# Moving the gate rows, the mask and the second block's loads, and splitting one weight tile earlier

## The chip, the cores and the metric

The kernel runs on one core of a Trainium2 chip. The metric is device time in microseconds (us) of one execution. The core's engines work side by side, each through its own instructions in program order: TensorE (PE, matmuls), VectorE (DVE), ScalarE (ACT), GpSimd (POOL, idle here), and SyncE (SP), which issues the loads. An instruction waits for those of other engines through semaphores.

## What is computed

Two transformer blocks in sequence over 256 tokens of width 1024, in float32. The first block:

```python
h = rmsnorm(x, norm1_g[l])
(hg_q, hg_f, hg_i, hg_g, ml_qk, ml_v, ml_if, ml_o,
 mb_z, mb_xbc, mb_dt, gate_pre) = jnp.split(h @ w_in[l], split_at, axis=-1)
log_f = jnp.log(lb + (1.0 - lb) * jax.nn.sigmoid(hg_f))
o_hg = hgrn2_scan(jax.nn.silu(hg_q), log_f, hg_i)
qk = jax.nn.silu(causal_dwconv(ml_qk, ml_conv_w[l], ml_conv_b[l]))
log_f_m = jax.nn.log_sigmoid(ml_if[..., 4:] + gb[4:])
h_ml = mlstm_scan(q_m, k_m * (ML_DQK ** -0.5), v_m, ml_if[..., :4] + gb[:4], log_f_m)
dt = jax.nn.softplus(mb_dt + mb_dt_bias[l])
y_ssd = ssd_scan(xs, dt, A, Bm, Cm)
mixed = gates[0] * (y_hg @ w_br_hg[l]) + gates[1] * (y_ml @ w_br_ml[l]) + gates[2] * (y_mb @ w_br_mb[l])
x = x + mixed @ w_out[l]
u = causal_dwconv(rmsnorm(x, norm2_g[l]) @ w_up[l], ffn_conv_w[l], ffn_conv_b[l])
u_g, u_v = jnp.split(u, 2, axis=-1)
x = x + (jax.nn.silu(u_g) * u_v) @ w_down[l]
```

The second block (two layers) has a context of 256 further tokens, a modulation by a condition vector, three kinds of mixing (one of them attention in a window, which needs a mask) and a feed-forward of the same kind. It uses the first block's x; its context and its layer parameters do not depend on the first block.

## The kernel before

Activations stand transposed, features on partitions: eight tiles of 128 x 256. Every weight matrix is cut into tiles of 128 x 1024. A tile is loaded (raw, 512 KB, four buffers, issued by SP), rounded to a high half on ACT (wh, L393) and to the rest on DVE (wl, L395), with three buffers for each half. A product is then 24 matmuls of 128 x 256, in threes: high by high (L414), high weight by low activation (L416), low weight by high activation (L417); where the activations are the stationary side the three are L439 to L441 (psx).

In the order of the program (a scheduler then sorts the instructions by it and by what they wait for, and each engine keeps the order that results):

- The start: x is loaded, normed (`rms_feat`), and while the norm is not there yet the first three tiles (`small`, hf0, hf1) are multiplied with the gain-scaled x (gh, gl) and scaled afterwards (`scaled`, L747, u). `normed` (L732) makes h and splits it into xh and xl (L400, L401), which all later tiles use. `small` holds the gate columns of the mLSTM and of the SSD; U is made of them.
- `small_rows` (L786 to L801) makes softplus (SP) and its scan (CS) from U, with a series for the logarithm: two ACT instructions and 17 on DVE, each over 128 x 256. It is called after the first step of `proj_a`, and CS and SP are first used in the mLSTM and the SSD, long after. Behind it the window mask is loaded and cast to `winb` (L1214).
- `run_ratio` runs the projections `proj_a` (hq, hi), `proj_b` (mqk, mv, xbc) and `proj_c` with the first scan, `hgrn_core`, a step of each in turn. A step of `proj_b` for mqk is one weight tile, a convolution (`conv4`, L923: an ACT row and three DVE rows cv) and a silu (`silu2`, L837: mq or hq from a tanh th). A step of `hgrn_core` makes decays E (L879 to L886), four pairs of psl matmuls, and takes them into AT (L901).
- Then the branches, the output product and the first feed-forward: 22 pairs of up tiles (j from 0), each followed by a convolution (ag, av, L641), a silu and a product. Its first four tiles (j below `raws` = 2) are again multiplied with gain-scaled x and scaled later (u, L1363), after which `normed` makes XH and XL. `hook1(j)` is called after every j; from j = 9 it takes a step of `context_norm`: modulation steps, `prepare(0)` (tables of the second block's first layer from its parameters plt), the context's norm.
- Between the weights run the modulation's steps: weight-like tiles reduced on DVE (L596), and tiles multiplied on PE (psada, L551, L552) whose rows are copied (arow) and turned (psat, L538).

The context (ctxT, eight loads of 128 KB) is loaded ahead of the first block's last branch; plt (588 KB) in `prepare`, when its pool is free.

Of the kernel before, what the change touches and what calls it, by code (L numbers as in the profile page):

```python
# [287 lines left out]
class Knobs:  # L288
    raw = 4
# [17 lines left out]
def tile_two_blocks(ctx: ExitStack, tc: tile.TileContext, xT, ctxT, cst1, cst, cstw, pb1, pl0, pl1, pf0, pf1, pc, pcb, wb, w0, w1, out,  # L307
# [55 lines left out]
    def load_params(pool, spec, src, nm):  # L363
        off, n = _poffs(spec)
        t = pool.tile([128, n], F32, name=nm)
        nc.sync.dma_start(out=t, in_=src)
        return lambda k: t[:, off[k][0]:off[k][0] + off[k][1]]
# [253 lines left out]
    def ffn(ph, pool, halves, xh, xl, cw3, cb, causal, resid, hook=None, mid=None, raw=None, raws=1):  # L621
# [6 lines left out]
        def part(c):  # L628
            return lambda k: (xh[:, k, c], xl[:, k, c])
# [23 lines left out]
        for j0, j1 in CHUNKS:  # L653
            hid = []
            for j in range(j0, j1):
                if j == 0 and raw:

                    ks, ps, us = [(i, e) for i in range(raws) for e in range(2)], [], []
                    for i, k in enumerate(ks):
                        if i >= 3:  # L660
                            us.append(raw[1](ps[i - 3]))
                        ps.append(gemm_ws(ph, ("up",) + k, raw[0], raw[3]))
                    us += [raw[1](p) for p in ps[len(us):]]
                    raw[2]()
                    pg, pv = us[0:2]
                elif j < raws and raw:
                    pg, pv = us[2 * j:2 * j + 2]
                elif j == 0:

                    w = [weight(ph, ("up", e // 2, e % 2), 128) for e in range(3)]  # L670
                    first = [PS.g.tile([128, 512], F32, tag=PS.gtag, name="psg") for _ in range(3)]
                    for c in reversed(H):
                        for e, ps in enumerate(first):
                            mm3(ps[:, c], w[e], part(c), 8, True)
                    pg, pv, pg1 = first
                elif j == 1 and not raw:
                    pg = pg1
                else:
                    pg = gemm_ws(ph, ("up", j, 0), part(slice(0, n)), n)
# [10 lines left out]
                if hook:  # L690
                    hook(j)
# [60 lines left out]
    uf = [scaled(gemm_ws(0, ("hf", j), graw, 256)) for j in range(2)]  # L752
    normed(xh, xl, x, r, g1[:, 0:8])
    dump("h", xh)
# [9 lines left out]

    lbe = p1.tile([128, 8], F32, name="lbe")
# [3 lines left out]
    S.activation(out=lbe, in_=lbe, func=AF.Exp)  # L769
    lbs = p1.tile([128, 8], F32, name="lbs")  # L770
# [11 lines left out]
    def small_rows():  # L782

        z = mid.tile([128, 256], F32, tag="E", name="z", bufs=4)
        s = mid.tile([128, 256], F32, tag="E", name="s", bufs=4)
        s2 = mid.tile([128, 256], F32, tag="E", name="s2", bufs=4)  # L786
        p = mid.tile([128, 256], F32, tag="E", name="p", bufs=4)
# [143 lines left out]
    def proj_b():  # L931
        for j in range(8):
            ps = gemm_ws(0, ("mqk", j), rhs, 256)
            silu2(mq[:, j * 256:(j + 1) * 256], conv4(ps, P("mcw"), P("mcb"), j))
            yield
# [273 lines left out]
    small_rows()  # L1209
    V.tensor_copy(identb, ident)  # L1210
    V.tensor_copy(causb, C("causal"))
    win = mid.tile([128, 512], F32, tag="E", name="win", bufs=4)
    nc.sync.dma_start(out=win, in_=cstw)
    V.tensor_copy(winb.rearrange("p a b -> p (a b)"), win)  # L1214
# [48 lines left out]
    cx = load_x(res2, ctxT, tag="cx")  # L1263
# [15 lines left out]
    def prepare(i):  # L1279
# [3 lines left out]
        P = L.P = load_params(lp, _pl(i), (pl0, pl1)[i], "plt")  # L1283
# [61 lines left out]
    def context_norm():  # L1345
        ada_steps(max(0, 32 - Ada.done))
        LS[0] = prepare(0)
        yield
        r = rms_feat(cx)
        yield  # L1350
        yield from norm_steps(LS[0], cx, r, 0, 1)
# [3 lines left out]
    def hook1(j):  # L1355
        if j >= 9:
            next(cn, None)

# [38 lines left out]
    def layer(L):  # L1397
# [366 lines left out]
        else:  # L1764
# [7 lines left out]
            def hook(j):  # L1772
# [53 lines left out]
```

## Time and profile before

| | before |
|---|---|
| median of three runs | 1729.18 us |
| the runs | 1727.62 to 1729.49 us |
| the profiled execution | 1728.11 us |
| its span in the profile | 1726.3 us |
| granted TensorE clock, mean of the span | 0.991 |
| busy: PE, DVE, ACT | 1680.2, 1422.8, 943.0 us |
| DMA | 278 MB, 161 GB/s in the mean |

The span runs from the first to the last recorded instruction; 1.8 us of the execution lie outside it. PE is busy for 97% of the span, DVE for 82%. A busy share says little about a place: at each, what counts is which engine waits and what ended its wait.

### The profile page before, as it was taken

Reading aid. Unit: us, or ns where it says so; the run is one execution under the profiler, and the core shown is the slowest. Engines: PE = TensorE matmul, PEld = TensorE weight load, DVE = VectorE, ACT = ScalarE, POOL = GpSimd, SP = SyncE. Lnnn points to the kernel's source line nnn. Section 1 sums busy time; section 2 is a strip of 40 time slices with the busy share of each in tenths; the row PEclk is TensorE's granted clock in tenths of the full one; section 3 lists DMA queues with packets and bytes.
Section 4 is the critical chain, followed back from the end, with each engine's and each line's share of the span. In section 5 each row is a group of like instructions: output and inputs, shape, how many; then the busy total and the mean of one; then the engine's idle time right before and its main releaser. Section 6 shows DMA issues by size and latency. Waiting matters only on the chain.

```text
span 1726.3 us, 31575 instructions
## 1 busy us (share of the span) xinstructions
PE 1680.2 (97%) x12334; PEld 1529.8 (89%) x12334; DVE 1422.8 (82%) x2788; ACT 943.0 (55%) x1661; POOL 0.2 (0%) x4
## 2 busy tenths in 40 slices
PE   7999999999999999999999999999999998899999
PEld 7999998889898999989877988888888996799999
DVE  8987977668789987876788899999997868688776
ACT  7655644444456665666777553431244555576454
POOL 0000000000000000000000000000000000000000
PEclk9999999999999999999999999999999999999999
DMA  8545454536665677764311546657753542046564
GB/s 264 162 151 156 137 159 121 150 111 213 206 212 165 194 234 224 218 203 147 99 50 52 169 138 184 186 170 237 242 165 110 170 134 63 1 144 196 177 193 135
DMA packets 80645, 278.01 MB, mean 161 GB/s; under 512 B 9072, under 2 KB 13808, under 8 KB 80240
## 3 DMA queue, kind: packets, MB, share of 16 engines
q1 hardware_dynamic: 80496, 275.99, 52.1%
q8 instruction: 97, 1.59, 0.4%
q14 instruction: 52, 0.43, 0.1%
HBM read 274.91 MB, written 1.05 MB: 160 GB/s over the span
## 4 chain that ended last, share of the span: by engine, by line
PE 84%; DVE 10%; ACT 3%; DMA 2%; issue 1%; SPq 0%; ACTq 0%; DVEq 0%
PE psg L414 20%; PE psg L417 20%; PE psg L416 20%; PE psx L439 3%; PE psx L441 3%; PE psx L440 3%; DVE wl L395 3%; PE psc L1568 2%; PE psl L894 1%; PE psc L1607 1%; ACT wh L393 1%; PE pso L1629 1%; PE pso L1626 1%; DMA raw<-w 1%; ACT Pp L1587 1%
## 5 line engine op out<-in xcount | busy, mean ns | idle before, releaser
L393 ACT CAST wh<-raw 128x1024 fp32r<-128x1024 f32 (+1 forms) x439 | 453.3, 1037 | 514.3 <-PE psg L416 419.0
L395 DVE TENSOR_TENSOR wl<-raw,wh 128x1024 fp32r<-128x1024 f32 (+1 forms) x439 | 528.2, 1206 | 136.6 <-ACT wh L393 133.6
L414 PE MATMUL psg<-XH,wh 128*128 128x256 f32 (+1 forms) x1272 | 396.3, 314 | 4.7 <-ACT wh L393 3.8
L417 PE MATMUL psg<-XH,wl 128*128 128x256 f32 (+1 forms) x1272 | 395.0, 313 | 4.7 <-DVE wl L395 4.7
L416 PE MATMUL psg<-XL,wh 128*128 128x256 f32 (+1 forms) x1224 | 384.6, 315 | 0.9 <-DVE XL L1331 0.5
L414 PEld LDWEIGHTS psg<-XH,wh 128*128 128x128 f32 x1272 | 240.3, 190 | 23.3 <-ACT wh L393 5.9
L417 PEld LDWEIGHTS psg<-XH,wl 128*128 128x128 f32 x1272 | 240.6, 190 | 21.3 <-DVE wl L395 5.7
L416 PEld LDWEIGHTS psg<-XL,wh 128*128 128x128 f32 x1224 | 231.9, 190 | 17.6 <-issue 1.1
L414 PE MATMUL psg<-xh,wh 128*128 128x256 f32 x720 | 208.2, 289 | 1.3 <-ACT xh L400 1.3
L417 PE MATMUL psg<-xh,wl 128*128 128x256 f32 x720 | 205.3, 285 | 2.6 <-DVE wl L395 2.6
L416 PE MATMUL psg<-xl,wh 128*128 128x256 f32 x720 | 205.7, 286 | 0.6 <-DVE xl L401 0.6
L414 PE MATMUL psg<-hh,wh 128*128 128x256 f32 (+1 forms) x592 | 178.6, 303 | 0.2
L416 PE MATMUL psg<-hl,wh 128*128 128x256 f32 (+1 forms) x592 | 178.3, 302 | 0.0
L417 PE MATMUL psg<-hh,wl 128*128 128x256 f32 (+1 forms) x592 | 178.2, 302 | 0.0
L414 PEld LDWEIGHTS psg<-xh,wh 128*128 128x128 f32 x720 | 137.8, 191 | 4.9 <-issue 2.9
L417 PEld LDWEIGHTS psg<-xh,wl 128*128 128x128 f32 x720 | 137.7, 191 | 4.9 <-DVE wl L395 3.2
L416 PEld LDWEIGHTS psg<-xl,wh 128*128 128x128 f32 x720 | 138.1, 192 | 1.8 <-issue 1.0
L414 PEld LDWEIGHTS psg<-hh,wh 128*128 128x128 f32 x592 | 111.0, 188 | 7.3 <-ACT hh L400 1.1
L416 PEld LDWEIGHTS psg<-hl,wh 128*128 128x128 f32 x592 | 111.2, 188 | 5.7 <-DVE hl L401 0.2
L417 PEld LDWEIGHTS psg<-hh,wl 128*128 128x128 f32 x592 | 111.1, 188 | 5.1
L439 PE MATMUL psx<-wh,XH 128*128 128x256 f32 x384 | 110.2, 287 | 1.3 <-ACT wh L393 0.8
L441 PE MATMUL psx<-wl,XH 128*128 128x256 f32 x384 | 109.3, 286 | 0.6 <-DVE wl L395 0.4
(445 smaller groups left out, 3181.7 us busy)
## 6 DMA issues: line engine op xcount, KB each, us to landing
raw<-w SPq DMA_DIRECT2D x238, 512.0 KB, 4.1
raw<-wb SPq DMA_DIRECT2D x197, 512.0 KB, 4.3
araw<-w SPq DMA_DIRECT2D x56, 512.0 KB, 4.3
raw<-w SPq DMA_DIRECT2D x16, 384.0 KB, 3.3
raw<-wb SPq DMA_DIRECT2D x8, 384.0 KB, 4.0
xres<-xT SPq DMA_DIRECT2D x16, 128.0 KB, 4.3
ccb<-pcb SPq DMA_DIRECT2D x2, 1024.0 KB, 5.4
plt<-pl SPq DMA_DIRECT2D x2, 588.0 KB, 4.2
```

Of the source, the lines that this page charges most:

```text
L393: S.copy(wh[:, 0:sz], raw[:, 0:sz])
L395: V.tensor_tensor(wl[:, 0:sz], raw[:, 0:sz], wh[:, 0:sz], ALU.subtract)
L414: T.matmul(o, wh[:, k], xh, start=(first and k == 0), stop=False)
L416: T.matmul(o, wh[:, k], xl, start=False, stop=False)
L417: T.matmul(o, wl[:, k], xh, start=False, stop=(last and not late and k == nk - 1))
L439: T.matmul(o, xh, wh[:, k % 4], start=(k == 0), stop=False)
L440: T.matmul(o, xl, wh[:, k % 4], start=False, stop=False)
L441: T.matmul(o, xh, wl[:, k % 4], start=False, stop=(k == 7))
L894: T.matmul(ps[:, a, t], E[:, o:o + 128], E[:, o:o + 128], start=True, stop=True)
L1568: T.matmul(ps[e][:, 0:A.nk], q_[d, jq, A.tq], k_[d, jk, kk], start=(n == 0), stop=(n == 2 and not mask))
L1587: S.activation(out=p[:, 0:A.nk], in_=o, func=AF.Exp, scale=ss[:, A.t, h:h + 1], bias=nm, accum_out=sums[:, c:c + 1])
L1607: T.transpose(ps[:, n], p[:, b * 128:(b + 1) * 128], ident)
```

## The change

- The start: hf0 and hf1 are multiplied as before; hf1 is scaled only behind `normed`. A single sigmoid (`sg0`) is called before the others.
- `small_rows` is called in `proj_b`, at the fifth mqk tile, and takes its four tiles from the pool of tmp instead of mid.
- The window mask is loaded in two halves and cast in `hook1`, at j = 6 and 7.
- The context is loaded in `hook1` at j = 4, behind a small ACT copy that writes a column of its tile from av; plt likewise behind a small ACT copy.
- In the first feed-forward the weight tile of j = 2 (the fifth) is asked for before the first four products are scaled (`ahead`).
- `hook1` takes one modulation step more at j = 12, 15 and 18.

```diff
-    def load_params(pool, spec, src, nm):
+    def load_params(pool, spec, src, nm, gate=None):
+        if gate is not None:
+            S.copy(t[:, 0:1], gate[:, 0:1])
         nc.sync.dma_start(out=t, in_=src)
...
                         ps.append(gemm_ws(ph, ("up",) + k, raw[0], raw[3]))
+                    ahead = weight(ph, ("up", raws, 0), 128)
                     us += [raw[1](p) for p in ps[len(us):]]
                     raw[2]()
...
-                    pg = gemm_ws(ph, ("up", j, 0), part(slice(0, n)), n)
+                    pg = gemm_ws(ph, ("up", j, 0), part(slice(0, n)), n, w=ahead if raw and j == raws else None)
...
-    uf = [scaled(gemm_ws(0, ("hf", j), graw, 256)) for j in range(2)]
+    uf = [gemm_ws(0, ("hf", j), graw, 256) for j in range(2)]
+    uf[0] = scaled(uf[0])
     normed(xh, xl, x, r, g1[:, 0:8])
+    uf[1] = scaled(uf[1])
...
+    S.activation(out=sg0, in_=ones, func=AF.Sigmoid)
...
-        z = mid.tile([128, 256], F32, tag="E", name="z", bufs=4)
...
+        z, s, s2, p = (tmp.tile([128, 256], F32, tag="t256", name=nm, bufs=6) for nm in ("z", "s", "s2", "p"))
...
     def proj_b():
         for j in range(8):
+            if j == 4:
+                small_rows()
             ps = gemm_ws(0, ("mqk", j), rhs, 256)
...
     next(pa)
-    small_rows()
...
-    win = mid.tile([128, 512], F32, tag="E", name="win", bufs=4)
-    nc.sync.dma_start(out=win, in_=cstw)
-    V.tensor_copy(winb.rearrange("p a b -> p (a b)"), win)
...
-    cx = load_x(res2, ctxT, tag="cx")
+    cx = res2.tile([128, 8, 256], F32, name="xres", tag="cx")
...
-        LS[0] = prepare(0)
+        LS[0] = prepare(0, gate[0])
...
+    def hook1(j, av):
+
+        gate[0] = av
+        if j in (6, 7):
+            win = tmp.tile([128, 256], F32, tag="t256", name="win", bufs=6)
+            nc.sync.dma_start(out=win, in_=cstw[:, (j - 6) * 256:(j - 5) * 256])
+            V.tensor_copy(winb[:, j - 6], win)
+        if j == 4:
+            S.copy(cx[:, :, 0:1], av[:, 0:8].unsqueeze(2))
+            for k in range(8):
+                nc.sync.dma_start(out=cx[:, k], in_=ctxT[:, k])
         if j >= 9:
             next(cn, None)
+        if j in (12, 15, 18):
+            ada_steps(1)
```

What this does to the order on DVE is shown at three places. In the rows an operation stands with what it writes and reads; line numbers of the changed kernel are 3 to 6 higher. The first place is the start, from the wl of the third hf tile on, before:

```order
L395 TENSOR_TENSOR wl<-raw,wh 128x1024
L747 TENSOR_TENSOR u<-psg,rr 128x256 x2
L760 TENSOR_SCALAR U<-u,pb1t,ct_125 128x256
L747 TENSOR_TENSOR u<-psg,rr 128x256
L732 SCALAR_TENSOR_TENSOR h<-xres,g_126,rr 128x256 x4
L401 TENSOR_TENSOR xl<-h,xh 128x256 x4
```

and in the changed kernel:

```order
L398 TENSOR_TENSOR wl<-raw,wh 128x1024
L751 TENSOR_TENSOR u<-psg,rr 128x256 x2
L736 SCALAR_TENSOR_TENSOR h<-xres,g_126,rr 128x256 x4
L766 TENSOR_SCALAR U<-u,pb1t,ct_125 128x256
L398 TENSOR_TENSOR wl<-raw,wh 128x1024
L404 TENSOR_TENSOR xl<-h,xh 128x256 x4
```

The four h come ahead of U and of the third u, and the wl of the fourth hf tile, which stood 16 rows behind these h, comes ahead of xl.

The second place is DVE from the wl of the last mqk tile to the wl of the first mv tile (the two wl rows here), before:

```order
L395 TENSOR_TENSOR wl<-raw,wh 128x1024
L837 SCALAR_TENSOR_TENSOR mq<-th,cv 128x256
L923 SCALAR_TENSOR_TENSOR cv<-psg,pb1t,cv 128x253
L886 TENSOR_TENSOR E<-E,hq 128x64x4
L923 SCALAR_TENSOR_TENSOR cv<-psg,pb1t,cv 128x254
L884 TENSOR_TENSOR E<-hb 128x128x2
L923 SCALAR_TENSOR_TENSOR cv<-psg,pb1t,cv 128x255
L901 COPY_PREDICATED AT<-ct_125,psl 128x2x256
L923 SCALAR_TENSOR_TENSOR cv<-psg,pb1t,cv 128x253
L837 SCALAR_TENSOR_TENSOR mq<-th,cv 128x256
L923 SCALAR_TENSOR_TENSOR cv<-psg,pb1t,cv 128x254
L395 TENSOR_TENSOR wl<-raw,wh 128x1024
```

In the changed kernel there are 35 rows between the two, the 17 of `small_rows` among them; the last of them are:

```order
L802 SCALAR_TENSOR_TENSOR p<-p,s_1453 128x256
L929 SCALAR_TENSOR_TENSOR cv<-psg,pb1t,cv 128x254
L803 SCALAR_TENSOR_TENSOR p<-p,s 128x256
L929 SCALAR_TENSOR_TENSOR cv<-psg,pb1t,cv 128x255
L805 SCALAR_TENSOR_TENSOR SP<-p,z 128x256
L907 COPY_PREDICATED AT<-ct_125,psl 128x2x256
L806 TENSOR_SCALAR z<-SP,acol 128x256
L843 SCALAR_TENSOR_TENSOR mq<-th,cv 128x256
L807 SCALAR_TENSOR_TENSOR CS<-ct_125,z 128x256
L929 SCALAR_TENSOR_TENSOR cv<-psg,pb1t,cv 128x253
L892 TENSOR_TENSOR E<-E,hq 128x64x4
L398 TENSOR_TENSOR wl<-raw,wh 128x1024
```

The E row of the level 64, which four pairs of psl matmuls read, is now the last but one of the 35, where it was the third of ten.

The third place is DVE in the body of the first feed-forward, where the context's norm begins (sacc, rcy, rct are its rows), between two wl rows, before:

```order
L395 TENSOR_TENSOR wl<-raw,wh 128x1024
L401 TENSOR_TENSOR hl<-av,hh 128x256
L459 TENSOR_TENSOR rct<-rct,psn 128x2
L596 ISA raw,mod_93<-raw,ccb,pf_575 128x1024
L596 ISA mod_93 128x1
L461 SCALAR_TENSOR_TENSOR rcy<-rct,rcy 128x2
L641 SCALAR_TENSOR_TENSOR ag<-psg,pb1t,ag 128x254
L457 TENSOR_TENSOR rct<-rcy 128x2
L395 TENSOR_TENSOR wl<-raw,wh 128x1024
```

The same stretch of the changed kernel has 40 rows between the two wl (those marked x2 counted twice); it begins with

```order
L457 TENSOR_SCALAR rcy<-psn 128x2
L398 TENSOR_TENSOR wl<-raw,wh 128x1024
L644 SCALAR_TENSOR_TENSOR av<-psg,pb1t,av 128x254
L1279 TENSOR_SCALAR g5n1g<-plt 128x8
L1297 TENSOR_SCALAR gtbqn<-plt 128x64
L1297 TENSOR_SCALAR gtbkn<-plt 128x64
L1280 SCALAR_TENSOR_TENSOR gs<-mod_93,g5n1g 128x16
L1298 TENSOR_TENSOR ctbqn<-ct,gtbqn 128x128
L1304 TENSOR_TENSOR stbqn<-ct,gtbqn 128x4x16 x2
```

and all rows of `prepare` now stand in it; before, a first half of them stood ahead of the fifth up tile's wl and a second half four wl rows ahead of this place.

## Rows read from the trace of the kernel before

**Rows 1.** The page's part 4, the chain that ended last, share by engine.

```profile
PE 84%; DVE 10%; ACT 3%; DMA 2%; issue 1%; SPq 0%; ACTq 0%; DVEq 0%
```

**Rows 2.** Timeline of PE at the start: start, duration, instruction, [idle before <- what ended it].

```profile
21.98 0.50 PE L414 MATMUL psg<-xh,wh 128*128 128x256 f32 x2 [1.35 <-ACT xh L400]
...
29.31 0.39 PE L417 MATMUL psg<-xh,wl 128*128 128x256 f32 x1 [1.43 <-DVE wl L395]
...
53.35 1.16 PE L869 MATMUL psl<-hq,hk 128*128 128x128 f32 x8 [1.54 <-DVE hq L837]
```

**Rows 3.** Timeline of DVE and of ACT at the start.

```profile
21.02 1.66 DVE L732 SCALAR_TENSOR_TENSOR h<-xres,g,rr 128x256 f32<-128x256 f32 x4
...
52.54 0.43 DVE L1214 CAST winb<-win 128x512 bf16<-128x512 f32 x1 [0.72 <-DMA win<-cstw]
52.89 0.75 DVE L837 SCALAR_TENSOR_TENSOR hq<-th,psg 128x256 f32<-128x256 f32 x2
...
51.21 1.02 ACT L836 ACTIVATE th<-psg 128x256 f32<-128x256 f32 x3
```

**Rows 4.** Timeline of DVE, rows of `small_rows` at their place before.

```profile
31.27 1.74 DVE L791 RECIPROCAL s<-s 128x256 f32<-128x256 f32 x1
...
46.61 3.17 DVE L796 SCALAR_TENSOR_TENSOR p<-p,s 128x256 f32<-128x256 f32 x7
```

**Rows 5.** Timeline of DVE from the last mqk tile's wl to the first mv tile's.

```profile
118.57 1.22 DVE L395 TENSOR_TENSOR wl<-raw,wh 128x1024 fp32r<-128x1024 f32 x1
119.71 0.42 DVE L837 SCALAR_TENSOR_TENSOR mq<-th,cv 128x256 f32<-128x256 f32 x1
120.04 0.48 DVE L923 SCALAR_TENSOR_TENSOR cv<-psg,pb1t,cv 128x253 f32<-128x253 f32 x1
120.43 0.42 DVE L886 TENSOR_TENSOR E<-E,hq 128x256 f32<-128x256 f32 x1
...
121.96 0.75 DVE L901 COPY_PREDICATED AT<-ct,psl 128x512 f32<-128x512 uint32 x1
...
123.75 1.22 DVE L395 TENSOR_TENSOR wl<-raw,wh 128x1024 fp32r<-128x1024 f32 x1
```

**Rows 6.** Timeline of PE, the first instruction behind the last mqk tile.

```profile
128.32 1.05 PE L894 MATMUL psl<-E 128*128 128x128 f32 x8
129.13 0.36 PE L439 MATMUL psx<-wh,xh 128*128 128x256 f32 x1
```

**Rows 7.** Busy time by stretch; PEclk is the granted clock.

```profile
28.00:33.00 5.00, 3.69 (x31) 3.69 (x32) 5.00 (x10) 4.55 (x10) 0.00 (x0) 1.00 0.46 136
...
142.00:160.00 18.00, 18.00 (x153) 17.90 (x152) 9.58 (x14) 8.77 (x15) 0.00 (x0) 1.00 0.54 153
544.50:549.50 5.00, 4.60 (x26) 4.60 (x27) 5.00 (x10) 2.31 (x8) 0.00 (x0) 0.66 0.63 156
```

**Rows 8.** Timeline of PE at the first feed-forward's head and behind its body.

```profile
544.90 0.45 PE L417 MATMUL psg<-XH,wl 128*128 128x256 f32 x1 [2.97 <-DVE wl L395]
...
741.79 0.28 PE L538 MATMUL psat<-ct,arow 4*128 4x4 f32 x2 [1.37 <-ACT arow L563]
```

**Rows 9.** Timeline of DVE at that head: the fifth up tile's wl, the sixth's.

```profile
532.34 1.22 DVE L395 TENSOR_TENSOR wl<-raw,wh 128x1024 fp32r<-128x1024 f32 x1
533.48 0.75 DVE L1363 TENSOR_TENSOR u<-psg,rr 128x256 f32<-128x256 f32 x2
...
543.63 1.22 DVE L395 TENSOR_TENSOR wl<-raw,wh 128x1024 fp32r<-128x1024 f32 x1
```

**Rows 10.** Timeline of DVE (a row of `prepare`; the body's wl) and of PE.

```profile
530.91 0.28 DVE L1294 TENSOR_TENSOR ctbqn<-ct,gtbqn 128x128 f32<-128x128 f32 x1
...
602.51 1.22 DVE L395 TENSOR_TENSOR wl<-raw,wh 128x1024 fp32r<-128x1024 f32 x1
...
603.78 0.39 PE L417 MATMUL psg<-XH,wl 128*128 128x256 f32 x1 [0.29 <-DVE wl L395]
```

**Rows 11.** The page's part 6: loads, KB each, us from issue to landing.

```profile
plt<-pl SPq DMA_DIRECT2D x2, 588.0 KB, 4.2
```

More of the change, by code (lines that the diff above doesn't have):

```diff
@@ L690, in ffn @@
                 if hook:
-                    hook(j)
+                    hook(j, av)
             if halves == 2 and j1 == NFF:
@@ L763, in tile_two_blocks @@
     V.tensor_scalar(acol, acol, -1.0, None, ALU.mult)
+    sg0 = p1.tile([128, 1], F32, name="sg0")
     lbe = p1.tile([128, 8], F32, name="lbe")
@@ L782, in small_rows @@
     def small_rows():
-        z = mid.tile([128, 256], F32, tag="E", name="z", bufs=4)
-        s = mid.tile([128, 256], F32, tag="E", name="s", bufs=4)
-        s2 = mid.tile([128, 256], F32, tag="E", name="s2", bufs=4)
-        p = mid.tile([128, 256], F32, tag="E", name="p", bufs=4)
+        z, s, s2, p = (tmp.tile([128, 256], F32, tag="t256", name=nm, bufs=6) for nm in ("z", "s", "s2", "p"))
         S.activation(out=z, in_=U, func=AF.Abs)
@@ L1277, in gains, with prepare @@
                                ALU.add, ALU.mult)
-    def prepare(i):
+    def prepare(i, gate=None):
         L = Layer()
         L.i = i
-        P = L.P = load_params(lp, _pl(i), (pl0, pl1)[i], "plt")
+        P = L.P = load_params(lp, _pl(i), (pl0, pl1)[i], "plt", gate)
         lami = 0.8 - 0.6 * math.exp(-0.3 * i)
@@ L1353, in tile_two_blocks @@
     cn = context_norm()
-    def hook1(j):
+    gate = [None]
+    def hook1(j, av):
[8 more added lines that the diff above has]
+                nc.sync.dma_start(out=cx[:, k], in_=ctxT[:, k])
         if j >= 9:
             next(cn, None)
+        if j in (12, 15, 18):
+            ada_steps(1)
     fp = b1.enter_context(tc.tile_pool(name="ffn1", bufs=2, side="right"))
@@ L1770, in layer, with hook @@
             Ada.pace, Ada.steps, Ada.done = Knobs.pace2, chain(ada_dve(0, 2, True), ada_dve(1, 2, True)), 0
-            def hook(j):
+            def hook(j, _):
                 if j == 13:
```

## The prediction

> **What bounds the kernel now.** I read the page's chain of work first: TensorE (PE) holds 84% of it, VectorE (DVE) 10% [rows 1]. So the time is PE's work plus the places where PE stands still. DVE matters because every weight tile passes through it: the subtraction on L395 makes the low half wl, and PE cannot take the third matmul of a tile before it is done. DVE executes in program order, so what is put ahead of a wl delays PE as soon as the lead is used up. I then looked in the timeline of PE for pauses and for what ended each, and in the timeline of DVE for what stood ahead there. A price is taken start to start: a conv row printed .48 takes .39, the next one starting .09 before its end [rows 5].
>
> **Start, gate rows gone.** Before, PE waits 1.35 us for the first xh, then for the first xl, 1.43 for the wl of the fourth hf tile (hf3), 1.54 for hq [rows 2]. In the changed order the h rows come 1.5 us sooner, but a U row (.33) and hf3's wl (1.14) are now ahead of xl, so the first xl comes when it did and the first two waits stay. PE now runs hf2 and hf3 side by side, so two hf3 matmuls (.24) fill the first wait and the 1.43 at 29.31 goes: 1.7 us. hq stood behind the gate rows and the mask cast winb, which waited .72 for its DMA [rows 3]. Without them it follows its tanh, the first of three that take 1.02 from 51.21 [rows 3], so at about 51.6 instead of 52.89: 1.2 of the 1.54 goes, at most all. Start: **-2.9** (range -2 to -4). Two activation table loads leave ScalarE there; PE's waits do not end on them, so they count nothing.
>
> **Gate rows at their new place.** They now lie in the order between the wl of the last mqk tile and the wl of the first mv tile, and the order packs 35 DVE rows between these two, where before there were 10. Of the 35, 17 are gate rows. The reciprocal takes 1.66 (printed 1.74) and the other 16 about .33 each, since each now alternates with a row that does not depend on it; in a chain, seven of them took 3.17, .45 each [rows 4]. That makes 6.9. The rest: 4 mq at .33 = 1.3, 11 conv rows at .39 = 4.3, 2 copies into AT at .65 (printed .75) = 1.3, 1 E row .33 [rows 5]. Sum 14.2 us. The first of them starts at 119.71 [rows 5], so the mv wl starts at 133.9 instead of 123.75 and ends at 135.1; the E row, the last but one, ends at 133.5. PE is done with the last mqk tile at 128.32 [rows 6]; in the changed order it then has four psx matmuls (.47) and asks for E at 128.8. It stands 4.7 us, does 8 psl matmuls (.8), stands .8 for the wl. Then 22 matmuls (2.6) cover the next wl, 2.5 later. Wait: **+5.5**. It is 4 if DVE gains a little lead and 7.5 if the 16 rows cost .45. What is behind: DVE works only 9.58 of the 18 us after 142 [rows 7], so the backlog is gone soon, but PE's loss is not handed back, since it is never ahead of its own work.
>
> [...]
>
> **The clock after a wait.** After the wait of 2.97 at 544.90 [rows 8] PE's granted clock is .66 over 5 us, and 26 matmuls take 4.60 busy us where 39 would fit (153 in 18.00): 13 x .118 = 1.5 us lost. After the wait of 1.43 at 29.31 the clock is 1.00 [rows 7]. A wait of 4.7 is beyond both, so I count **+1.5** (0 to 1.5). [...]
>
> **First feed-forward, head.** DVE does 27 rows (scaled products, h, XL, conv) before the wl that ends at 544.85, started at 543.63, and PE stands 2.97 [rows 8, 9]. The tile split early is the fifth, whose wl already stood ahead of these rows; the one PE waits for is the sixth, and in the changed order the same 27 rows are still ahead of it. The 12 small preparing rows that leave cost DVE little and the fifth tile's high half is not there sooner: **-0.1**, up to -0.5.
>
> **First feed-forward, body.** The layer's preparation moves later, and its parameters load later. In the changed order ahead of the wl that started at 602.51 [rows 10] there is: 24 preparing rows, the longest .2 (printed .28) and most a fraction of its size, 2.5; a modulation reduction 1.2; six conv rows 2.3; two products .7; norm rows .8; and the wl before it 1.14: 8.6 us, where before there were 3.3. The wl before it can come some 2.8 sooner, since those rows were ahead of it. It cannot use more, because the norm row just ahead waits for PE. So this wl starts at about 605.0, 2.5 later. PE is waiting for it already in the kernel before, .29 at 603.78 [rows 10], so lateness counts nearly in full: PE ends that tile **1.8** later (its norm and modulation matmuls now run inside the wait). PE's wait is some 3.5 us, more than the 2.97, so another **+1.5** for the clock. Range of both: 0 to 6. The first preparing row waits for the parameter load, 4.2 us after its issue [rows 11], and the load now waits for a ScalarE copy late in the loop; by my count it lands at the moment it is asked for, with that wl queued behind it. The eight context loads (1 MB) now go between weight loads on SP's queue, five squares on ScalarE wait for them, and the high half of a weight tile stands behind these: I find about 1 us of lead left, and count zero. Both are in the range above.
>
> **First feed-forward, tail.** Three of six modulation tiles leave the tail, where PE waits 1.37 for a row copy [rows 8], for the loop's body. What they take is the same in either place, one of them inside the wait above, and the norm's sums now stand ahead of the matmuls. I take **-1.5**, bounds 0 and -2.8 (twice that wait).
>
> **Sum.** -2.9 + 5.5 + 1.5 - 0.1 + 1.8 + 1.5 - 1.5 = +5.8. The profiled execution took 1728.1, 1.8 outside its span among it, 1.1 under the median of the runs. 1728.1 + 5.8 = 1733.9; I take 1734.0.
>
> **The rivals.**
> *The clock does not fall.* The two long waits cost only themselves, as at 29.31: -3.0, 1731. For it: a wait is not always followed by half rate [rows 7]. Against: both waits are longer than the one that was.
> *No wait at the gate rows.* PE asks for E 9.1 us after the first of the 35 rows; if DVE has them behind it by then, because with 8 us less work at the start it runs further ahead, the 7.0 go: 1727, not slower than before. It decides from 13.5 us of rows ahead of E down to 9.1. Against it: the conv rows among them wait for PE's own tiles and the wl for free buffers, so DVE cannot run ahead by 4 us.
> *Late loads.* The parameters or the context land some 4 us late, one raw load's time, with a wl or a high half queued behind: 1738. For it: the two gates leave no lead; against: raw loads are asked for four tiles ahead.
> *The early split works.* The 27 rows turn out not to hold PE, 2.97 + 1.5 go: 1729.5. Against: the order.
>
> **How the numbers follow.** Forecast .50 (1731.5 to 1736), clock .15, no wait .12, late loads .13, early split .10. This kernel's measurement tells about 0.2% from no change, so faster is below 1725.7 and slower above 1732.6. Slower: .50 x .85 + .13 = .55. Same: the rest of the forecast .08, the clock .15, early split .08, half of no wait .05, .35 with rounding. Faster: what is left, .10, cases in which the 7.0 go and the start gains its full 4. With .1 left out on either side the range is 1726.5 to 1739.
>
> **What would show it.** Right: a PE wait of 4 to 5 us on psl just before the first mv tile, ended by an E row; a clock under 1 after it; no waits at 29 and little before hq; the wait of some 3 us at the sixth feed-forward tile still there; a wait of 3 to 4 us about 60 us later, ended by a wl or by the norm's rcy. Wrong: DVE idle among the gate rows, PE busy through there, or a raw load as what ends PE's chain in the loop.

## The result and the profile after

| | before | changed |
|---|---|---|
| median | 1729.01 us (11 runs) | 1738.64 us (11 runs) |
| the runs | 1721.96 to 1731.24 | 1732.62 to 1746.82 |
| ratio to before, 95% interval | | 1.0061 (1.0045 to 1.0076) |
| the profiled execution, its span | 1728.11, 1726.3 | 1732.62, 1730.8 |
| granted clock of the profiled execution | .991 | .990 |
| granted clock, mean over the runs | .990 (25 further runs) | .985 |

The change makes the kernel slower, by 0.61%, some 10.5 us of 1728. The forecast was 1734.0, +4.8 against the median of three runs. The direction was right; what came is twice as much.

The execution that was profiled is the fastest of the eleven, with a clock of .990, only 4.5 us above the profiled one of before. So its trace shows where the new waits are, but not all that they cost; the clock in the other runs does, and the experiments have to share it out.

Three readings of the trace after. First PE's timeline (start, duration, instruction, idle before and what ended it), at the places that the prediction names and at those that it does not:

```profile
21.84 0.50 PE L417 MATMUL psg<-xh,wh 128*128 128x256 f32 x2 [0.71 <-ACT xh L403]
23.82 0.58 PE L419 MATMUL psg<-xl,wh 128*128 128x256 f32 x1 [1.47 <-DVE xl L404]
...
31.99 0.39 PE L417 MATMUL psg<-xh,wh 128*128 128x256 f32 x1 [0.80 <-ACT hk L816]
...
51.71 1.16 PE L875 MATMUL psl<-hq,hk 128*128 128x128 f32 x8 [0.61 <-DVE hq L843]
...
128.97 0.36 PE L442 MATMUL psx<-wh,xh 128*128 128x256 f32 x1 [1.91 <-DVE cv L929]
...
131.81 2.05 PE L900 MATMUL psl<-E 128*128 128x128 f32 x8 [2.37 <-DVE E L892]
...
525.72 0.38 PE L478 MATMUL psn<-onesn,sacc 128*128 128x1 f32 x2 [1.35 <-DVE sacc L486]
...
544.90 0.39 PE L420 MATMUL psg<-XH,wl 128*128 128x256 f32 x1 [2.98 <-DVE wl L398]
...
578.74 0.39 PE L420 MATMUL psg<-XH,wl 128*128 128x256 f32 x1 [0.94 <-DVE wl L398]
...
603.92 0.36 PE L417 MATMUL psg<-XH,wh 128*128 128x256 f32 x1 [1.04 <-DVE ag L644]
...
606.62 0.71 PE L495 MATMUL psr<-ct,rcy 128*128 128x128 f32 x4 [2.23 <-DVE rcy L464]
...
752.48 0.39 PE L442 MATMUL psx<-wh,XH 128*128 128x256 f32 x1 [1.32 <-ACT wh L396]
...
768.22 0.58 PE L444 MATMUL psx<-wl,XH 128*128 128x256 f32 x1 [2.71 <-DVE wl L398]
...
1509.05 0.63 PE L1625 MATMUL psc<-ct,Pp 128*128 128x128 f32 x4 [2.22 <-DVE Pp L1614]
```

At the start the wait for the fourth hf tile's wl [rows 2] is gone and the one for hq has fallen from 1.54 to 0.61. The wait before the first mv tile is there, in two pieces, one ended by a conv row cv and one by E. The sixth feed-forward tile waits as before, 2.98 against 2.97 [rows 8]. The body has its two long waits at 603.92 and 606.62. And at 768.22 PE waits 2.71 for a wl, which no step of the prediction had.

Then busy time by stretch (PE busy and count, weight loads, DVE, ACT, POOL, granted clock, DMA):

```profile
400.00:418.00 18.00, 18.00 (x161) 18.00 (x160) 12.09 (x18) 9.36 (x14) 0.00 (x0) 1.00 0.69 232
544.50:549.50 5.00, 4.60 (x26) 4.61 (x27) 5.00 (x10) 1.98 (x6) 0.00 (x0) 0.66 0.64 165
...
129.00:134.00 5.00, 2.63 (x12) 2.46 (x13) 4.69 (x11) 0.60 (x2) 0.00 (x0) 0.55 0.00 0
134.00:139.00 5.00, 5.00 (x37) 5.00 (x36) 3.96 (x6) 1.61 (x4) 0.00 (x0) 0.77 0.74 206
...
526.00:531.00 5.00, 5.00 (x45) 5.00 (x46) 4.13 (x10) 1.24 (x2) 0.00 (x0) 1.00 0.67 229
607.00:612.00 5.00, 4.88 (x28) 4.39 (x28) 4.82 (x8) 1.40 (x4) 0.00 (x0) 0.66 0.75 219
...
768.20:773.20 5.00, 4.98 (x30) 4.99 (x31) 2.23 (x2) 1.43 (x3) 0.00 (x0) 0.70 0.72 238
...
1509.00:1514.00 5.00, 4.28 (x35) 4.07 (x36) 1.76 (x9) 1.00 (x2) 0.00 (x0) 1.00 0.00 0
```

The clock drops below 1 behind four of the long waits: the one at 131.81, the one at 606.62, the one at 768.22, and the old one at 544.90 [rows 7]. Behind the shorter one at 525.72 it stays at 1.00, and also behind one of 2.22 in the second block, at 1509.05; at the same place in the kernel before, behind a wait of 2.22 too, it was .66 over the 5 us from 1502.70. So a long wait is not always followed by a fall. The .66 of the 5 us is a mean: read by half microseconds behind the wait at 544.90, the granted clock is 1.00 over 545.0 to 545.5, .50 from 546.0 to 549.0 and 1.00 again over 549.5 to 550.0.

Last the DVE rows at the gate rows' place, from the last mqk tile's wl to the first mv tile's:

```profile
118.08 0.42 DVE L843 SCALAR_TENSOR_TENSOR mq<-th,cv 128x256 f32<-128x256 f32 x1
...
126.56 0.43 DVE L802 SCALAR_TENSOR_TENSOR p<-p,s 128x256 f32<-128x256 f32 x1
126.89 0.48 DVE L929 SCALAR_TENSOR_TENSOR cv<-psg,pb1t,cv 128x253 f32<-128x253 f32 x1
...
131.25 0.42 DVE L892 TENSOR_TENSOR E<-E,hq 128x256 f32<-128x256 f32 x1
...
131.97 1.22 DVE L398 TENSOR_TENSOR wl<-raw,wh 128x1024 fp32r<-128x1024 f32 x1
```

The stretch from the first row to the wl takes 131.97 - 118.08 = 13.9 us, where the sum said 14.2. DVE is busy for all 13.89 of it.

### The profile page after: what moved, and what is told of

It is laid out like the page before. It is cut to its first block, busy times and chain, and to the rows that moved or that the text cites. A ratio compares the mean times of both kernels' runs of the same rounds, so it can differ in the third digit from the quotient of the medians.

```text
span 1730.8 us, 31598 instructions
## 1 busy us (share of the span) xinstructions
PE 1672.2 (97%) x12334; PEld 1519.3 (88%) x12334; DVE 1421.3 (82%) x2789; ACT 941.6 (54%) x1663; POOL 0.2 (0%) x4
## 4 chain that ended last, share of the span: by engine, by line
PE 53%; DVE 6%; ACT 3%; issue 1%; DMA 0%; DVEq 0%; ACTq 0%; SPq 0%
PE psg L417 13%; PE psg L420 13%; PE psg L419 13%; PE psx L442 3%; PE psx L444 3%; PE psx L443 2%; PE psc L1586 2%; DVE wl L398 1%; PE psc L1625 1%; PE pso L1647 1%; PE pso L1644 1%; ACT wh L396 1%; ACT Pp L1605 1%; DVE h L1333 1%; DVE mx L1599 1%
```

## The experiments

Each kernel was timed beside the kernel before, so ratios are compared, and a difference in ratio is turned into us by 1728. Where two such ratios are subtracted, the difference carries some 0.002, or 3.5 us, either way. A run's mean granted clock is given where it bears on a step; time lost to the clock is worked out as mean time x (1 - mean clock), which is at most what it costs, since the low clock of stretches in which PE stands still is counted too (.50 over 130 to 131 us in the changed kernel, with PE busy for 0.00).

### The gate rows

e1 is the kernel before with `small_rows` at its new place alone. e2 is the changed kernel with `small_rows` back.

```diff
+            if j == 4:
+                small_rows()
...
-    small_rows()
```

> The kernel before, with only small_rows called at the fifth mqk tile (its four tiles from tmp); mask, loads, start and feed-forward as before. Theory A (the packed gate rows hold PE): between the last mqk wl and the first mv wl stand 35 DVE rows as in the changed kernel, so PE waits 4 to 5.5 us there, the clock falls after it, the hq wait at the start shortens by some 1.2; in all +5, about 1734. Theory B (the backlog is absorbed, the loss of the changed kernel lies in its feed-forward): no wait over 1 us there, 1728 to 1729.

> The changed kernel with small_rows back at its old place and tiles; everything else changed. Theory A: the waits of 1.9 and 2.4 us ahead of the first mv tile go, and the half-clock stretch after them; about 6 less than the changed kernel (1738.6), some 1 given back at the start: 1733 to 1734. Theory B: no better than the changed kernel, 1738 to 1739.

e1: 1731.84 us, ratio 1.0020 (1.0010 to 1.0031), +3.5 us. e2: 1734.27, ratio 1.0034 (1.0019 to 1.0048); the step back is worth 0.0027, 4.7 us. Alone and inside the change, the gate rows cost some 4 us, less than the 5 of theory A for e1. The trace of e1 has the same two waits, without any other part of the change:

```profile
130.52 0.36 PE L439 MATMUL psx<-wh,xh 128*128 128x256 f32 x1 [1.88 <-DVE cv L920]
...
133.37 0.91 PE L891 MATMUL psl<-E 128*128 128x128 f32 x4 [2.37 <-DVE E L883]
```

The second is the wait for E of the prediction. The first is a piece of the same lateness that I had not placed: the third of the four psx matmuls needs a psum buffer (the memory that this kernel's matmuls write to) that a conv row among the 35 has to empty first. Together they are 4.25 us, where the sum had 4.7 for E. So the place, the engine and the size of the wait are shown. In e1's trace the clock is .77 and .89 in the two 5 us stretches from 131 on; the mean clock of its runs is .990, as before, so this one drop does not show in the mean. The wait for hq at the start is gone in e1, but psl starts at 53.26, hardly before the 53.35 of the kernel before [rows 2]: moving the gate rows alone gave nothing back there.

### The start, and 32 bytes

e4 is the kernel before with the new start alone: hf1 scaled behind `normed`, and `sg0`.

```diff
+    uf = [gemm_ws(0, ("hf", j), graw, 256) for j in range(2)]
+    uf[0] = scaled(uf[0])
     normed(xh, xl, x, r, g1[:, 0:8])
+    uf[1] = scaled(uf[1])
...
+    sg0 = p1.tile([128, 1], F32, name="sg0")
+    S.activation(out=sg0, in_=ones, func=AF.Sigmoid)
```

> The kernel before with only the start changed: hf1 scaled behind the norm and the early sigmoid. Theory A: the wait of 1.4 us for hf3's wl goes, the first xl wait grows by what the xh wait loses; -1 to -1.7: 1727.5 to 1728. Rival: hf3's rows ahead of xl only move the wait, 1729.

e4: 1722.59 us, ratio 0.9973 (0.9962 to 0.9984), -4.7 us. That is more than the trace of its start gives: with the gate rows still there, the psl matmuls that wait for hq start at 53.45, against 53.35 before [rows 2]. So the gain lies elsewhere. Matmuls of equal shape stand closer together in it from 130 to some 530 us. The built programs explain what is different: `sg0` takes 32 bytes of each partition in the pool p1, and with it xh moves from byte 192160 of the partition to 192128, xl from 200352 to 200320, and hh likewise. Before, these addresses left a rest of 32 when divided by 64; now they are multiples of 64. Two kernels test the address alone. f5 is the kernel before with an unused pad of the same size, f6 the changed kernel with `sg0` 64 bytes wide, so that the addresses leave a rest of 32 again.

```diff
+    pad = p1.tile([128, 1], F32, name="pad")
+    V.memset(pad, 0.0)
```

```diff
-    sg0 = p1.tile([128, 1], F32, name="sg0")
+    sg0 = p1.tile([128, 16], F32, name="sg0")
-    S.activation(out=sg0, in_=ones, func=AF.Sigmoid)
+    S.activation(out=sg0[:, 0:1], in_=ones, func=AF.Sigmoid)
```

> The kernel before with one tile more, of one float per partition, cleared once: it takes 32 bytes, as sg0 does in the changed kernel, and moves xh, xl and the feed-forward's hh, hl down by 32 bytes, so that they begin at a multiple of 64. No other instruction changes. Theory M (PE reads an operand that begins at a multiple of 64 bytes faster: 113 us per thousand matmuls instead of 118): the spacing of matmuls between 150 and 730 us falls from 118 to 113 to 116 ns and the time by 4 to 5: 1723 to 1724. Theory S (the gain of the start alone, -5, is from its reordering): 1727 to 1729, spacing 118.

> The changed kernel with sg0 made 16 floats wide (64 bytes instead of 32), so that xh, xl, hh and hl begin 32 bytes behind a multiple of 64 as in the kernel before. Theory M: spacing back at 118 ns, 3 to 5 more than the changed kernel: 1742 to 1744. Theory S: the same as the changed kernel, 1738 to 1739.

f5: 1724.71 us, ratio 0.9983 (0.9968 to 0.9997), -2.9 us. f6: 1742.02, ratio 1.0090 (1.0071 to 1.0108), 0.0029 or 5.0 us above the changed kernel. Busy time by stretch shows it in the traces, in 18 us without a wait. The kernel before:

```profile
400.00:418.00 18.00, 18.00 (x155) 18.00 (x154) 13.54 (x21) 9.06 (x14) 0.00 (x0) 1.00 0.70 221
```

f5, the pad alone:

```profile
400.00:418.00 18.00, 18.00 (x161) 18.00 (x161) 12.77 (x18) 8.37 (x14) 0.00 (x0) 1.00 0.63 207
```

f6, the changed kernel off the multiple of 64:

```profile
400.00:418.00 18.00, 18.00 (x154) 18.00 (x153) 14.58 (x24) 9.70 (x16) 0.00 (x0) 1.00 0.73 231
```

With a granted clock of 1.00 in all of them, 161 matmuls run with the operands on a multiple of 64 (the changed kernel has 161 too) and 154 or 155 without: 111.8 ns each against 116.1 and 116.9. XH and XL of the feed-forward are a check on that. The pad does not move them: XH starts at byte 91968, a multiple of 64, in all of these kernels, and the pieces of it that PE reads do so too. Yet their matmuls keep the wider spacing. f5 again, in a stretch that has these alone:

```profile
553.00:571.00 18.00, 18.00 (x154) 18.00 (x153) 17.84 (x30) 12.15 (x20) 0.00 (x0) 1.00 0.64 209
```

The kernel before and the changed kernel have 154 in this stretch as well, f6 has 152. So the matmuls that got closer are those whose tiles moved, but a start at a multiple of 64 is not enough by itself; what else it takes is open.

So 3 to 5 us of gain came with the change by an accident of where tiles lie, and they are no part of what the prediction priced. Part of the closer spacing is lost again in waits. The changed kernel, which comes sooner to the norms, waits 2.30 for rqy, the row that a norm of the first block needs:

```profile
457.54 1.99 PE L1166 MATMUL psr<-rqy,ct 4*128 4x256 f32 x8 [2.30 <-DVE rqy L464]
```

f6, which differs from it by the address alone, waits less at that place:

```profile
461.24 1.99 PE L1166 MATMUL psr<-rqy,ct 4*128 4x256 f32 x8 [0.70 <-DVE rqy L464]
```

The wait of 1.35 for sacc at 525.72 is of the same kind: f6 has none above 0.3 there.

h1 has the other half of the new start, the order without `sg0`.

```diff
-    uf = [scaled(gemm_ws(0, ("hf", j), graw, 256)) for j in range(2)]
+    uf = [gemm_ws(0, ("hf", j), graw, 256) for j in range(2)]
+    uf[0] = scaled(uf[0])
     normed(xh, xl, x, r, g1[:, 0:8])
+    uf[1] = scaled(uf[1])
```

> The kernel before, only with hf1 scaled behind normed; no sg0, so xh, xl and hh keep the addresses that they had. Theory S (the reorder gains by itself): the start with sg0 gained 5.2 us of the median, the 32-byte shift alone 3.1, so the reorder is worth some 2: 1725 to 1726.5, spacing of the matmuls of 128x256 at 300 to 450 us still 118 ns. Rival (the whole gain of the new start was the address): within 1 us of the kernel before, 1727 to 1729.

h1: 1725.65 us, ratio 0.9982 (0.9974 to 0.9991), -3.1 us, with 154 matmuls in 400 to 418 us. By its time theory S holds, but the trace does not carry it:

```profile
23.07 0.50 PE L414 MATMUL psg<-xh,wh 128*128 128x256 f32 x2 [0.61 <-ACT xh L400]
24.26 0.38 PE L416 MATMUL psg<-xl,wh 128*128 128x256 f32 x1 [0.69 <-DVE xl L401]
...
28.90 0.38 PE L417 MATMUL psg<-xh,wl 128*128 128x256 f32 x1 [0.70 <-DVE wl L395]
...
53.62 1.16 PE L871 MATMUL psl<-hq,hk 128*128 128x128 f32 x8 [1.71 <-DVE hq L839]
```

The waits for xh and for hf3's wl fall, the one for xl grows from 0.58 to 0.69, the hq wait grows from 1.54 to 1.71, and psl starts at 53.62, not sooner than before: what PE gains at the first tiles it gives back at hq, which stands behind the gate rows and the mask's cast on DVE. The mean clock of h1's runs is .9915 against .9892 of the runs of before beside it, which is worth up to 4 us and could be all of the gain. Whether the order raises the clock, and by what, stays open; single runs differ by as much.

### The loads

e3 is the changed kernel with both loads where they were before; h3 only frees plt of its copy, the context keeps its own.

```diff
-    cx = res2.tile([128, 8, 256], F32, name="xres", tag="cx")
+    cx = load_x(res2, ctxT, tag="cx")
...
-        LS[0] = prepare(0, gate[0])
+        LS[0] = prepare(0)
...
-        if j == 4:
-            S.copy(cx[:, :, 0:1], av[:, 0:8].unsqueeze(2))
-            for k in range(8):
-                nc.sync.dma_start(out=cx[:, k], in_=ctxT[:, k])
```

(h3 has the line of `prepare` alone.)

> The changed kernel with the context's load ahead of the third branch again and the layer's parameters loaded without a gate; gate rows, mask, start and the three extra modulation steps as changed. Theory A (the preparing rows packed behind the late load hold PE in the loop): the 40 DVE rows ahead of one wl become 9 to 13, the waits of 1.0 and 2.2 us near 603 go, with the half-clock stretch after them; 3 to 4 less than the changed kernel: about 1735. Theory C (the loads cost nothing, the gate rows and the tail are the loss): 1738 to 1739.

> The changed kernel, only with the parameters plt loaded without the ScalarE copy ahead; the context still waits for its copy at j = 4. Theory P (as predicted: it is the preparing rows, late because of plt, that delay the wl at 602 us): as with both loads back, 1733 to 1734.5, and the waits of 1.0 and 2.2 us at 602 to 605 us gone. Rival X (the context's loads and the squares on ScalarE behind them): as the changed kernel, 1737.5 to 1740, waits at 577 and 602 to 605 us still there.

e3: 1733.65 us, ratio 1.0034 (1.0021 to 1.0046), 0.0027 or 4.7 us better than the changed kernel. h3: 1735.92, ratio 1.0041 (1.0025 to 1.0057), 0.0020 or 3.5 us better, which is not clear of noise. In e3's trace the body has two waits above 0.3 left:

```profile
594.51 0.39 PE L420 MATMUL psg<-XH,wl 128*128 128x256 f32 x1 [0.82 <-DVE wl L398]
...
602.39 0.39 PE L420 MATMUL psg<-XH,wl 128*128 128x256 f32 x1 [0.64 <-DVE wl L398]
```

In h3's the wait for rcy is gone, and short ones for ag and wl are left:

```profile
580.98 0.36 PE L417 MATMUL psg<-XH,wh 128*128 128x256 f32 x1 [0.96 <-DVE ag L644]
...
603.84 0.39 PE L420 MATMUL psg<-XH,wl 128*128 128x256 f32 x1 [0.52 <-DVE wl L398]
```

So the wait of 2.23 for the norm's rcy hangs on plt's gate: with it, the order has the preparing rows late, ahead of the rcy chain and of the wl behind it. The time of h3 lies between the two theories, and its interval overlaps both; how the rest divides between plt and the context is not settled.

### The extra modulation steps

e6 is the changed kernel without the three steps in the loop, h2 the kernel before with them alone.

```diff
+        if j in (12, 15, 18):
+            ada_steps(1)
```

> The changed kernel without the three extra modulation steps at j = 12, 15 and 18. Theory D (with these steps the norm behind the feed-forward is late on DVE; the wait of 2.7 us for a wl at 765 and the half-clock stretches around it come from there): that wait falls below 1, the mean granted clock rises from .985 towards .990, 3 to 6 less: 1733 to 1735. Rival (the tail only moves, the lower clock has another source): 1738, clock .985.

> The kernel before, only with the three modulation steps more at j = 12, 15 and 18. Theory D (the steps moved out of the tail cost by themselves, since three wl then stand together behind the rows of the second norm): slower by 4 to 6 us, 1732 to 1734, with a wait of 2 to 3 us at a psx <- wl near 765 us, as the changed kernel has it. Rival (as predicted, the tail gets shorter): faster by 0 to 2, 1726 to 1728; the loss that went away with the steps in the changed kernel came from the steps together with the late loads.

e6: 1733.23 us, ratio 1.0039 (1.0024 to 1.0053), 0.0022 or 3.8 us better than the changed kernel. h2: 1734.94, ratio 1.0040 (1.0028 to 1.0052), +6.9 us against before. A step that I had booked as a gain of 1.5 is a loss, and by h2 the dearest part of the change. DVE's timeline of the kernel before shows where, in the second norm's rows ahead of the second block:

```profile
760.67 1.28 DVE L1329 SCALAR_TENSOR_TENSOR h<-xres,gx,rr 128x256 f32<-128x256 f32 x3 [0.95 <-ACT rr L494]
...
765.42 0.87 DVE L1329 SCALAR_TENSOR_TENSOR h<-xres,gx,rr 128x256 f32<-128x256 f32 x2
766.22 1.22 DVE L395 TENSOR_TENSOR wl<-raw,wh 128x1024 fp32r<-128x1024 f32 x1
...
768.14 2.35 DVE L395 TENSOR_TENSOR wl<-raw,wh 128x1024 fp32r<-128x1024 f32 x2
```

h2's DVE at the same place:

```profile
759.94 1.67 DVE L1329 SCALAR_TENSOR_TENSOR h<-xres,gx,rr 128x256 f32<-128x256 f32 x4 [2.61 <-ACT rr L494]
...
764.70 1.67 DVE L1331 SCALAR_TENSOR_TENSOR XL<-h,mod,XH 128x256 fp32r<-128x256 f32 x4
766.28 3.49 DVE L395 TENSOR_TENSOR wl<-raw,wh 128x1024 fp32r<-128x1024 f32 x3
```

And what PE does there in h2:

```profile
747.93 0.28 PE L538 MATMUL psat<-ct,arow 4*128 4x4 f32 x2 [0.45 <-ACT arow L563]
750.73 0.58 PE L439 MATMUL psx<-wh,XH 128*128 128x256 f32 x1 [1.32 <-ACT wh L393]
...
767.55 0.58 PE L441 MATMUL psx<-wl,XH 128*128 128x256 f32 x1 [2.70 <-DVE wl L395]
```

Before, one wl stands among the sixteen rows of h and XL, and PE waits only 0.39 for it. With three steps fewer in the tail the order has all sixteen rows ahead of three wl in a row, and PE waits 2.70 for the first. The two XL rows that now come ahead of it are 0.8 of the difference of 2.3. The larger part is that PE has less to do meanwhile: the norm's rows now come two weight tiles sooner, and between the norm's psr and this wait PE runs 44 psx matmuls in h2, 5.6 us, where it ran 56, 7.1 us, before. The wait for arow falls as forecast, from 1.37 to 0.45; the wait for wh next to it grows from 0.83 to 1.32, and the new one takes 2.7. In e6's trace the wl stands among those rows again and the wait of 2.7 is gone, while the two in the body (0.92 and 2.22) remain: the two losses are separate. Up to half of h2's loss may be the clock: its five runs have .9874 in the mean against .9892 of before beside them, 1735.2 x .0126 - 1729.1 x .0108 = 3.2 us, and around the wait of 2.70 its clock is .66:

```profile
766.00:771.00 5.00, 3.44 (x16) 3.45 (x17) 3.77 (x4) 0.72 (x2) 0.00 (x0) 0.66 0.38 137
```

### A version that beats both

g1 is the kernel before with the pad, `small_rows` at the third mv pair, and the mask in two halves at the third and fourth. h4 is g1 with the new start instead of the pad (hf1 behind `normed`, and `sg0`); loads, split and modulation steps stay as before.

```diff
         for c in range(4):
+            if c == 2:
+                small_rows()
+            if c > 1:
+                win = tmp.tile([128, 256], F32, tag="t256", name="win", bufs=6)
+                nc.sync.dma_start(out=win, in_=cstw[:, (c - 2) * 256:(c - 1) * 256])
+                V.tensor_copy(winb[:, c - 2], win)
             gemm_xs(0, [("mv", c, 0), ("mv", c, 1)], lhs, (0, 1),
```

> The kernel before with the pad of 32 bytes, small_rows called at the third mv pair and the mask in two halves at the third and fourth mv pair; loads, feed-forward and the start's order as before. The order spreads the gate rows over six wl, 2 to 9 DVE rows between two. Theory A with M: no wait over 1 us around the mv tiles, the hq wait of 1.5 near 52 falls below .5, the spacing 113 to 116: 1721 to 1722, less than the pad alone. Rival (DVE's idle time there is not free: rows packed anywhere hold a wl): 1724 or more.

> The kernel before with the gate rows and the mask behind the third and fourth mv pair, as in the run before this one with the pad, and with the start of the changed kernel (hf1 scaled behind normed, sg0 in place of the pad): loads and modulation steps stay as before. Theory S: the reorder adds its 2 us to the 5.4 of late rows and pad, 1720 to 1721, less if both shorten the same wait before hq. Rival: the two share the same gain and add nothing, 1722 to 1723.

g1: 1722.33 us, ratio 0.9975 (0.9959 to 0.9990). h4: 1720.73, ratio 0.9959 (0.9947 to 0.9971), -7.1 us: faster than before and 1% faster than the changed kernel. The mv stretch has room for the gate rows: in h4 PE is never short of work there, at a clock of 1.00, while DVE does them.

```profile
126.00:144.00 18.00, 18.00 (x157) 18.00 (x156) 17.92 (x37) 10.23 (x19) 0.00 (x0) 1.00 0.50 161
```

And at the start psl begins 2.4 us sooner than before [rows 2], which the new order alone (h1) did not bring:

```profile
50.99 1.16 PE L871 MATMUL psl<-hq,hk 128*128 128x128 f32 x8 [0.61 <-DVE hq L839]
```

That is not shown to be due to the gate rows. The mask's cast, which stood ahead of hq and waited 0.72 for its load [rows 3], is gone from there too. And e2, which has the new start and the cast in the feed-forward but the gate rows at their old place, begins psl as soon, in an execution whose clock did not fall at the start:

```profile
51.08 1.16 PE L878 MATMUL psl<-hq,hk 128*128 128x128 f32 x8 [1.28 <-DVE hq L846]
```

How much of it is the gate rows', the cast's or the clock's is open.

What h4 adds to g1 (0.0016) lies inside both intervals, so it is not told from nothing. The same holds for what g1 adds to the pad alone (f5, 0.0008). That the mv stretch takes the gate rows without a wait is in the trace; how much of the 7.1 us comes from it, from the mask, the order or the address is not.

## Why the prediction had the sign and half the size

The parts, as measured, against the steps of the prediction:

| step | forecast, with its clock | measured |
|---|---|---|
| start | -2.9 | -4.7 alone (e4), of which -2.9 (f5) to -5.0 (f6) the address |
| gate rows | +5.5 and +1.5 | +3.5 alone (e1), +4.7 (e2) |
| head, early split | -0.1 | the wait is 2.98 against 2.97 |
| body: loads and preparation | +1.8 and +1.5 | +4.7 (e3) |
| extra steps, tail | -1.5 | +6.9 alone (h2), +3.8 (e6) |
| all | +5.8 | +10.5 |

The three parts measured alone and the loads add up to 3.5 - 4.7 + 4.7 + 6.9 = 10.4, close to the whole. That is no proof that nothing is missing: each number in it carries 2 to 4 us of its own uncertainty, with e6 in place of h2 the sum is 7.3, and the mask was not run by itself.

**Gate rows.** Right in mechanism, place and length. 35 rows took 13.9 us, and PE waited 4.3 instead of the 4.7 for E. The row p at 126.56 is followed by its neighbour at 126.89, .33 later; by the price of the chain, .45, the 16 rows would have taken 2 us more than the 13.9. So the two prices of the rows, .33 and .45, were the right choice against one price for all. What e1 and e2 measured, 3.5 and 4.7, is about the wait alone; the 1.5 for the clock behind it is in the traces (.55 and .77 over the two stretches from 129) but not on top in the times.

**Start.** Half right. The wait for the fourth hf tile's wl went, as said; but the step "the first two waits stay" failed. The h rows come 0.7 sooner (20.31 against 21.02 [rows 3]), not 1.5; U and hf3's wl still stand ahead of xl, so the wait for xh falls to 0.71 and that for xl grows to 1.47, from 0.58. A new one of 0.80 at 31.99 is ended by hk, which ScalarE makes from a product. At psl, where all of this ends, the changed kernel is 1.64 us ahead of before (51.71 against 53.35), not 2.9. e4, in the table, still has the gate rows and the mask ahead of hq, so no run measures this step by itself.

**The address.** Not in the prediction at all. It gave back 3 to 5 us, so the steps that I did price cost 13 to 15 us, not 10.5. The error of the total hides a larger one of its parts, and the total would have missed by more without this luck.

**Head.** Right: the tile that waits is the sixth, and the 27 rows are still ahead of it. Built without the early split, the program has the instructions of PE, DVE, ACT and SP in the same order, so the split changes nothing that runs.

**Body.** Right in mechanism and in the trace: the forecast wait of some 3.5 us came as 1.04 + 2.23 + 0.12, the longest piece ended by the norm's rcy, with a clock of .66 behind it. Under-sized, if anything: the wait of 0.94 at 578.74 before it was not seen, and the whole part costs 4.7 where 3.3 were booked, a difference inside e3's own error.

**Tail.** This is the step that failed, and it failed by sign: -1.5 was booked, and the runs have +6.9 alone (h2) and +3.8 inside the change (e6). I priced what leaves the tail (a row copy's wait) and not what stands closer together when it has left: the order, which I had read at three places and not at this one, has the norm's rows two weight tiles sooner there, all sixteen ahead of three wl, and PE waits 2.7 for a wl instead of 0.4. The bounds 0 and -2.8 excluded a loss without a reason for it. The difference between -1.5 and what e6 and h2 measured, 5 to 8 us, is by itself more than what the table misses, 10.5 - 5.8 = 4.7.

**The clock.** Counted at +3.0, for two waits. In the mean of the runs the loss to the clock is 1738.95 x .0149 = 25.9 us in the changed kernel and 1727.98 x .0102 = 17.6 in the 25 runs of before beside the first experiments, a difference of some 8 at most, which may be the larger part of the 10.5. The rule that I used, a long wait costs 1.5 again by the clock, was my estimate from one wait, the 2.97 at 544.90 [rows 7, 8]. In the trace after, the clock falls behind the long waits at 131.81, 544.90, 606.62 and 768.22 (.55, .66, .66 and .70 over 5 us), and not behind the one at 1509.05 (1.00). The same place can be followed by a fall in one execution and not in another: behind the wait of 2.22 in the second block the clock is .66 in the profile of before and 1.00 in that of the changed kernel. And the runs of the changed kernel range from a clock of .990 to .980, with times from 1732.6 to 1746.8. The mean clock is .986 to .987 in e2, e3, e6, f6, h2 and h3, and .989 to .991 in e1, e4, f5, g1, h1 and h4. The first six have the extra steps, the late loads or both, the others neither. Against the runs of before beside them, the loads without the steps lower it by .004 (e6) and the steps without the loads by .003 (e3), both with the moved gate rows and the mask; the gate rows alone do not (e1). The steps alone (h2) lower it by .0018, no more than the pad does (f5, .0016), so there it is not told from nothing. Which single wait does it is not shown. The trace after has a fall behind some waits and not behind every one: behind the wait of 2.71 at 768.22 the clock is .70, behind that of 1.35 at 525.72 it is 1.00, with 45 matmuls in 5 us.

**Rivals.** No wait at the gate rows fell by the trace (4.3 us). The clock not falling fell for the profiled execution (.55 and .66). Late loads was right that this part costs, and its 1738 near the measured time is luck, since it was not right about how: no raw load and no high half ends a wait in the body, the preparing rows do. The early split fell.

## What to carry to other kernels

Read the changed order at every place that an edit empties as well as at those that it fills: work taken out of a stretch lets other work close up, and the next wl can end up behind all of it. Small work that has no deadline belongs in a stretch where the trace shows DVE idle and PE full, as the mv pairs are here, and not where the last lead has just been used up. When a part gains more than its waits explain, look at where tiles lie in memory before looking for a mechanism, and try a pad by itself.

## What the runs showed of the hardware

The same matmuls of 128 x 256 in float32 ran closer together when the tiles of their moving operands (xh, yh and their low parts) were moved by 32 bytes, to a multiple of 64: 161 in 18.00 us against 155 and 154 at a clock of 1.00, 111.8 ns each against 116.1 and 116.9. One small tile more, which moves those behind it by 32 bytes, changed a kernel of 1728 us by 2.9 us (f5) and 5.0 us (f6). The kernels h1 and before, with the rest of 32, stand at 154 and 155. It is no rule for every tile: the matmuls of XH, at a multiple of 64 in all of these kernels, stay at 152 to 154. Only rests of 0 and 32 were tried.

The clock can fall although the profile shows no pause of PE. In the trace of before PE is busy without a break from 255 us on, and the clock falls at 275:

```profile
270.00:275.00 5.00, 5.00 (x34) 4.34 (x34) 4.79 (x17) 1.99 (x4) 0.00 (x0) 1.00 0.16 25
275.00:280.00 5.00, 5.00 (x30) 4.87 (x29) 3.99 (x9) 1.84 (x5) 0.00 (x0) 0.66 0.46 138
```

What PE did there, ahead of the fall, includes sixteen matmuls with a stationary side of eight columns (128*8):

```profile
265.22 3.62 PE L1137 MATMUL psn<-sq,nwin 128*8 128x256 f32 x16
```

In the profiled run of the changed kernel the clock over 275 to 280 us is 1.00; of the fourteen profiled executions four have a fall near there: .66 in before and in h2 and .72 in h3 over 275 to 280 us, .77 in g1 over 270 to 275. So the waits that I counted are not all that the clock answers to, and one execution does not tell what a place costs in the mean: eleven runs of the changed kernel had from .980 to .990, and 14 us went with it.
